# Row sums of transposed modulation weights on VectorE, and the gates' low halves moved from GpSimd to VectorE

## The chip, the cores and the metric

The kernel runs on one core of one Trainium2 chip. The metric is the device time of one execution in microseconds, the median of several runs. All input data are in HBM at the start, in the layouts that the host function `arrays` gives them; the host does no arithmetic.

## The reference, cut to what matters

Two diffusion blocks follow each other. Both scale, shift and gate their token streams by a modulation vector that is a product of a small activation with a wide matrix:

```python
silu_c = jax.nn.silu(c)
silu_cc = jax.nn.silu(c_ctx)[None]
for l in range(2):
    mod = silu_c @ w_ada[l] + b_ada[l]        # 1024 -> 6144, latent stream
    mod_c = silu_cc @ w_ada[l] + b_ada[l]     # the same for the context stream
    ...
    g = sigmoid(gate_cols)                    # 3 x 1024 columns of h @ w_in
    m = g[0]*(f_mix @ w_br_fourier) + g[1]*(o_g @ w_br_global) + g[2]*(o_w @ w_br_window)
    y = m @ w_out
    ...                                       # residual, then 16 experts
m_lat = jax.nn.silu(c_2) @ w_mod_2 + b_mod_2  # second block, 1024 -> 6144
```

In layer 1 the context stream needs only the first third of the modulation, and in the second block likewise, so for most of those two matrices only one of the two streams has to be modulated.

## The kernel before, in words

`build` runs `mixer(0)` (attention and branches of layer 0, both streams, 512 tokens), `moe(0)` (experts), `mixer(1)`, `moe(1)` and `block2`. A tile scheduler sets the order of the instructions on each engine when the kernel is built; the order in which the code issues them is the input to it.

Every weight matrix comes as blocks of 1 MB, [128, 2048] in fp32, into a ring of four raw buffers `w` (`raw`, line 176, and `wraw`, line 192). The loads stand in one queue, SyncE's, in the order in which the code asks for them, and a load starts only when the buffer four loads back has been read for the last time. Matrices that TensorE multiplies in two halves go through `halves` (line 180): ScalarE writes the high half `whi` (line 173), another engine the low half `wlo` as the difference (line 174). There are two buffer pairs for the halves, so a block is split while TensorE still works on the block before it. `mm3` (lines 163 to 165) then issues three matmuls per block of 128 rows.

Modulation comes in 36 chunks (m, c): matrix m (0 and 1 are the layers' `w_ada`, 2 is `w_mod_2`), columns 512c to 512c + 511. A chunk is two 1 MB loads. There are two ways to compute it:

- `mod_chunk` (line 263) on TensorE, for both streams.
- `mod_chunk_v` (line 285) on VectorE, for the latent stream alone. The weights lie with the input index on the partitions. Eight instructions on [128, 512] (one at line 298, seven at line 296) sum weight times activation into `modrow`, and four small matmuls against a column of ones (`one2`, issued through line 158) add over the partitions into a PSUM tile `sm`, of which there is a single one. Line 303 adds the bias.

`mixer(0)` gets a list `extra` of 32 chunks. Half of them run as fills between the steps of the two attentions, the other 16 in the strips of the branches: four strips jj, each with the gates (jj, 0..2), then a block of `wbr`, the branch products, and the merge on VectorE (lines 701 and 703). Four of the twelve gates, (0, 0), (0, 1), (0, 2) and (1, 0), are computed earlier, as fills in the attentions. Behind each gate's place some chunks are issued:

```python
load = [1 if x in early else 2 for x in order]
...
if (jj, i) not in early:
    gate(jj, i, nc.gpsimd if full else None)
n = 3 * jj + i
run_extra(round(len(extra) * load[n] / sum(load[n:])))
```

With `nc.gpsimd` the low halves of those eight gates are subtracted on GpSimd. Between the attentions and the strips stands `fourier` (line 542), a short chain of matmul, copy, matmul, copy. In front of the attentions stand five projections `proj` (line 397) of 256 columns each, from the blocks w_in 1024, 1280, 256, 512 and 768.

`bcast_cols` (line 317) spreads a column of 1024 values over all partitions as a row: eight matmuls against the identity (line 323) and two copies from PSUM (line 325).

Of the kernel before, what the change touches and what calls it, by code (L numbers as in the profile page):

```python
# [122 lines left out]
class Kernel:  # L123
# [89 lines left out]
    def setup(self):  # L213
        nc, tc, a = self.nc, self.tc, self.a
        st = self.st
        self.cp = st.enter_context(self.pool("consts"))
        self.pp = st.enter_context(self.pool("psum", space=PSUM))
        self.cw = {}
        nv = a["vecs"].shape[1]
        self.vec = self.cp.tile([128, nv], F32, name="vec")  # L220
        nc.sync.dma_start(self.vec, a["vecs"])
        self.ident = self.cp.tile([128, 128], F32, name="ident")
        nc.sync.dma_start(self.ident, a["ident"])
        self.ex = self.cp.tile([128, 1], F32, name="ex")
        nc.vector.memset(self.ex, -0.5)
        self.identb = self.cp.tile([128, 128], BF, name="identb")
        nc.vector.tensor_copy(self.identb, self.ident)
        self.ahead = {}
        self.one2 = self.cp.tile([128, 2], F32, name="one2")
        nc.vector.memset(self.one2, 1.0)  # L230
        self.modT = [self.cp.tile([128, 48, 2], F32, name=f"modT{i}") for i in range(3)]

        self.cst = []
        for i, nm in enumerate(("c", "c2")):
            c = self.V(nm).rearrange("p (s k) -> p s k", s=2)
            t = self.cp.tile([128, 2, KT], F32, name="silu")
            nc.scalar.activation(t, c, AF.Tanh, scale=0.5)
            nc.vector.scalar_tensor_tensor(t, t, 1.0, c, op0=OP.add, op1=OP.mult)
            s = self.cp.tile([128, KT, 32], F32, name=f"cst{i}")
            nc.vector.memset(s, 0.0)  # L240
            nc.vector.tensor_scalar(s[:, :, 0:2], t.rearrange("p s k -> p k s"), 0.5, None, op0=OP.mult)
            self.cst.append(s)
# [41 lines left out]

    def mod_chunk_v(self, m, c):

        nc = self.nc
        src = self.a["w_ada"][m] if m < 2 else self.a["w_mod_2"]
        st = self.cst[0 if m < 2 else 1]
        acc = self.mp.tile([128, 512], F32, name="modrow")  # L290
        for h in range(2):
            w = self.wraw(src[2 * c + h], 4, 512)
            for k in range(4):
                s = st[:, 4 * h + k, 0:1]
                if h or k:
                    nc.vector.scalar_tensor_tensor(acc, w[:, k], s, acc, op0=OP.mult, op1=OP.add)  # L296
                else:
                    nc.vector.tensor_scalar(acc, w[:, k], s, None, op0=OP.mult)
        pt = self.psum("sm", [128, 4, 2])
        for b in range(4):  # L300
            self.mm(pt[:, b], acc[:, b * 128:b * 128 + 128], self.one2, True, True)
        b = self.V("b_ada", m) if m < 2 else self.V("b_mod")
        nc.vector.tensor_tensor(self.modT[m][:, 4 * c:4 * c + 4], pt,
                                b[:, 4 * c:4 * c + 4].unsqueeze(2).to_broadcast([128, 4, 2]), op=OP.add)

    def mod_coef(self, m, i, gain, name, parts=1):
# [251 lines left out]
    def mixer(self, l, xsrc, extra):  # L558
# [9 lines left out]
        def run_extra(n):  # L568
            for _ in range(min(n, len(extra))):
                m, c = extra.pop(0)  # L570
                (self.mod_chunk_v if m and c >= 4 else self.mod_chunk)(m, c)

        gates = {}

        def gate(jj, i, eng=None):
            w = self.wsplit(a["w_in"][l, 6 + 4 * i + jj], eng)
            for j in range(2):
                ps = self.psum("pg")
                for k in range(KT):
                    self.mm3(ps[:, :N], [x[:, k, j * 128:j * 128 + 128] for x in w],  # L580
                             [h[:, k, :N] for h in self.hl], k == 0, k == KT - 1)
                g = gp.tile([128, N], F32, name="gate", bufs=8)
                nc.scalar.activation(g, ps[:, :N], AF.Tanh, scale=0.5)
                gates[jj, i, j] = g
# [1 line left out]

        early = [(0, 0), (0, 1), (0, 2), (1, 0)]
        fills = [lambda x=x: gate(*x) for x in early]
        at = len(extra) * 16 // 32
        for n in range(at):  # L590
            fills.insert(n * (len(fills) - n) // at + n, lambda: run_extra(1))
        rate = max(0, len(fills) - 2) / (6 * T)
# [33 lines left out]
        with self.pool(f"at{l}", side="right") as self.ap:  # L626
            self.consts(self.ap, _const_attn, "cattn")
            self.maskb = self.ap.tile([128, 256], BF, name="maskb")
            mask = self.ap.tile([128, 256], F32, name="mask", tag="rt2")
            nc.scalar.dma_start(mask, a["mask"])  # L630
            nc.vector.tensor_copy(self.maskb, mask)
            gq = self.ap.tile([128, 64], F32, name="gq")
            nc.gpsimd.dma_start(gq, a["q_norm_g"][l:l + 1].to_broadcast([128, 64]))
            gk = self.ap.tile([128, 64], F32, name="gk")
            nc.gpsimd.dma_start(gk, a["k_norm_g"][l:l + 1].to_broadcast([128, 64]))
            sink = self.ap.tile([128, 4], F32, name="sink")
            nc.gpsimd.dma_start(sink, a["sink"][l:l + 1].to_broadcast([128, 4]))
            z4 = self.ap.tile([128, T, 256], F32, name="z4")
            kvw = self.ap.tile([128, 4, 256], F32, name="kvw")
            heads = lambda x: x.rearrange("p t (h v d) -> p t h v d", v=2, d=64)  # L640
            qw = heads(z4)
            self.proj(l, 1024, lambda t: qw[:, t].rearrange("p h v d -> p v h d"), range(T))
            self.proj(l, 1280, lambda t: kvw[:, t], range(4))
            qv = z4.rearrange("p t (h d) -> p t h d", d=64)
            kv = kvw.rearrange("p t (h d) -> p t h d", d=64)
            for t in range(2):
                self.rope(qv[:, t], t)
                self.rope(kv[:, t, 0:2], t)
            qg = self.ap.tile([128, T, 512], F32, name="qg")
            qgh = heads(qg)  # L650
            kvg = self.ap.tile([128, 4, 256], F32, name="kvg")
            self.proj(l, 256, lambda t: qgh[:, t, :, 0], range(T))
            self.proj(l, 512, lambda t: qgh[:, t, :, 1], range(T))
            self.proj(l, 768, lambda t: kvg[:, t], range(4))
            self.attention(l, qw, kv, 2, T, lambda h, t: oT[:, 6 + h, t * 128:t * 128 + 128], fill, sink=sink)
            f = self.ap.tile([128, T, 256], F32, name="z4")
            self.proj(l, 0, lambda t: f[:, t], range(T))
            qv = qg.rearrange("p t (h d) -> p t h d", d=64)
            kv = kvg.rearrange("p t (h d) -> p t h d", d=64)
            for t in range(4):  # L660
                if t < T:
                    self.head_norm(qv[:, t], gq)
                self.head_norm(kv[:, t, 0:2], gk)
                if t < 2:
                    self.rope(qv[:, t], t)
                    self.rope(kv[:, t, 0:2], t)
            self.attention(l, qgh, kv, 4, T, lambda h, t: oT[:, 2 + h, t * 128:t * 128 + 128], fill)
            fill(len(fills))
            for s in range(S):
                self.fourier(f, s, lambda c: oT[:, c, s * 256:s * 256 + 256])  # L670
# [6 lines left out]
        with self.pool(f"br{l}", side="right") as bp:  # L677
# [1 line left out]
            for k in (6, 7, 2, 3, 4, 5, 0, 1):  # L679
                self.split(ol[0][:, k], ol[1][:, k], oT[:, k])  # L680
            order = [(jj, i) for jj in range(4) for i in range(3)]
            load = [1 if x in early else 2 for x in order]
            for jj in range(4):
                for i in range(3):
                    if (jj, i) not in early:
                        gate(jj, i, nc.gpsimd if full else None)
                    n = 3 * jj + i
                    run_extra(round(len(extra) * load[n] / sum(load[n:])))
                w = self.wsplit(a["wbr"][l, jj])
                for _ in range(EARLY[jj] if not full else 0):  # L690
                    self.load_expert(l, FIRST + len(self.pre))
# [1173 lines left out]
def _blocks(w, k, n):  # L1865


    *lead, r, c = w.shape
    m = len(lead)
    w = w.reshape(*lead, r // (128 * k), k, 128, c // n, n)  # L1870
    w = w.transpose(*range(m), m + 3, m, m + 2, m + 1, m + 4)
    return np.ascontiguousarray(w.reshape(*lead, -1, 128, k * n))
# [6 lines left out]

def _mod_blocks(w):  # L1880

    return np.concatenate([_blocks(w[:, :2048], KT, 256), _blocks(w[:, 2048:], 4, 512)])


def arrays(inp):
# [29 lines left out]
def build(tc, a, dbg=None):  # L1915
# [4 lines left out]
    k.wps, k.sps = [k.wp], [k.sp]  # L1920
    with k.pool("modp", bufs=2, side="right") as k.mp:
        k.mixer(0, [a["x"], a["ctx"]],
                     [(0, c) for c in range(4, 12)] + [(m, c) for r in (range(4), range(4, 12)) for m in (1, 2) for c in r])
    k.moe(0, 2, 2)
    k.dbg("xl0", k.X[0][:, 0])
    k.mixer(1, None, [])
# [23 lines left out]
```

## Time and profile before

| what | value |
|---|---|
| median of 3 runs | 2176.22 us (2176.04 to 2177.61) |
| the profiled execution | 2179.61 us, its span 2177.8 us |
| TensorE (PE) busy | 1911.4 us, 88% of the span, mean granted clock 0.92 |
| VectorE (DVE) busy | 986.0 us, 45% |
| ScalarE (ACT) busy | 546.9 us, 25% |
| GpSimd (POOL) busy | 115.5 us, 5% |
| DMA | 601.95 MB, mean 276 GB/s |
| costliest VectorE line of the chunks, L296 | 112 instructions, 105.4 us, mean 950 ns |

Busy shares are averages over the whole span. The layer-0 mixer takes the first quarter of it, and what a change there is worth has to be read from the windows, waits and timeline of that quarter. The granted clock is a share of full speed: 1.00 is 2.4 GHz, 0.50 is 1.2 GHz. PEld is the loading of weights into TensorE, which overlaps matmuls; PE's idle time in front of an instruction is given with what ended it.

### The profile page before, as it was taken

How to read it: one execution, taken by the hardware profiler on the slowest of the kernel's cores; microseconds unless marked ns; L12 is line 12 of the kernel's file. 1: busy time of each engine (PE TensorE's matmuls, PEld its weight loads, DVE VectorE, ACT ScalarE, POOL GpSimd, SP SyncE). 2: the span in 40 equal slices, each digit the busy share in tenths (PEclk: the TensorE clock that was granted, in tenths of full speed). 3: DMA queues.
4: the chain of work that ended last, by engine and by line, in shares of the span. 5: the costliest groups of instructions: out<-in, count | busy, mean ns of one | idle time of the engine just before them, and what ended most of it. 6: DMA issues, size and time to landing. Idle time of an engine off the chain costs nothing. (4 is left out here: it accounts for less than half of the span.)

```text
span 2177.8 us, 31443 instructions
## 1 busy us (share of the span) xinstructions
PE 1911.4 (88%) x13182; PEld 1288.5 (59%) x13182; DVE 986.0 (45%) x1907; ACT 546.9 (25%) x1076; POOL 115.5 (5%) x113
## 2 busy tenths in 40 slices
PE   5999999997999999787989977688876659998998
PEld 4967767886433343222968964354432228897997
DVE  3485688864222133123787642132221036855554
ACT  3144422231000110002344420131100014344342
POOL 0210013200000000000210000000000000100000
PEclk9999998998999989999999988888886778998999
DMA  8255766775799959999314669999899992313541
GB/s 331 76 217 212 271 232 251 283 298 203 296 421 420 410 223 420 420 421 385 135 59 155 239 232 418 419 391 421 338 416 420 417 393 98 117 59 121 187 177 59
DMA packets 85454, 601.95 MB, mean 276 GB/s; under 512 B 10048, under 2 KB 10848, under 8 KB 13376
## 3 DMA queue, kind: packets, MB, share of 16 engines
q1 hardware_dynamic: 82928, 594.15, 68.8%
q10 hardware_dynamic: 1840, 5.46, 0.7%
q8 instruction: 104, 1.70, 0.3%
q0 software_dynamic: 544, 0.32, 0.2%
q14 instruction: 38, 0.31, 0.0%
HBM read 598.84 MB, written 1.05 MB: 275 GB/s over the span
## 5 line engine op out<-in xcount | busy, mean ns | idle before, releaser
L158 PE MATMUL ps<-we 128*32 128x256 f32 (+2 forms) x2400 | 358.4, 528 | 88.1 <-DMA we<-w_up_e_dram 46.4
L158 PEld LDWEIGHTS ps<-we 128*32 128x32 f32 (+2 forms) x2400 | 124.5, 138 | 298.1 <-issue 118.2
L173 ACT CAST whi<-w 128x1024 fp32r<-128x1024 f32 x170 | 174.1, 1045 | 232.2 <-PE ps L164 110.0
L158 PE MATMUL ps<-we,gT 128*32 128x256 f32 (+1 forms) x1536 | 201.5, 494 | 30.7 <-DMA we<-w_down_e_dram 30.5
L174 DVE TENSOR_TENSOR wlo<-w,whi 128x1024 fp32r<-128x1024 f32 x154 | 185.8, 1220 | 84.7 <-ACT whi L173 84.1
L1022 DVE TENSOR_TENSOR we<-ps,we 32x512 f32<-32x512 f32 (+1 forms) x128 | 70.9, 554 | 209.4 <-PE ps L158 207.8
L158 PEld LDWEIGHTS ps<-we,gT 128*32 128x32 f32 (+1 forms) x1536 | 65.9, 126 | 140.5 <-issue 73.3
L163 PE MATMUL ps<-hhi,whi 128*128 128x512 f32 (+1 forms) x384 | 133.2, 347 | 0.1
L164 PE MATMUL ps<-hlo,whi 128*128 128x512 f32 (+1 forms) x384 | 132.5, 346 | 0.0
L165 PE MATMUL ps<-hhi,wlo 128*128 128x512 f32 (+1 forms) x384 | 131.6, 345 | 0.1
L296 DVE SCALAR_TENSOR_TENSOR modrow<-w,cst,modrow 128x512 f32<-128x512 f32 x112 | 105.4, 950 | 2.3
L158 PE MATMUL ps<-we,xg 128*32 128x256 f32 (+1 forms) x768 | 99.3, 484 | 5.3 <-DMA we<-w_gate_e_dram 3.6
L989 DVE TENSOR_TENSOR g<-tanh,ps 128x512 f32<-128x512 f32 (+1 forms) x32 | 17.7, 554 | 185.7 <-PE ps L158 185.6
L163 PE MATMUL ps<-hl,whi 128*128 128x256 f32 x352 | 100.6, 286 | 0.1
L165 PE MATMUL ps<-hl,wlo 128*128 128x256 f32 x352 | 99.9, 286 | 0.0
L164 PE MATMUL ps<-hl,whi 128*128 128x256 f32 x352 | 99.7, 285 | 0.0
L163 PE MATMUL ps<-whi,hhi 128*128 128x256 f32 x320 | 92.6, 291 | 2.5 <-DVE hhi L376 2.3
L986 ACT ACTIVATE tanh<-ps 128x512 f32<-128x512 f32 (+1 forms) x32 | 15.7, 490 | 312.0 <-PE ps L158 312.0
L164 PE MATMUL ps<-wlo,hhi 128*128 128x256 f32 x320 | 91.9, 289 | 0.9 <-DVE wlo L174 0.9
L987 DVE SCALAR_TENSOR_TENSOR tanh<-tanh,ps 128x512 f32<-128x512 f32 (+1 forms) x32 | 17.7, 554 | 165.3 <-ACT tanh L986 165.3
L165 PE MATMUL ps<-whi,hlo 128*128 128x256 f32 x320 | 91.2, 290 | 0.0
L210 POOL TENSOR_TENSOR rstd<-rstd,ex 128x2 f32<-128x2 f32 (+2 forms) x17 | 16.2, 954 | 1344.7 <-DVE rstd L342 1294.2
(423 smaller groups left out, 3557.9 us busy)
## 6 DMA issues: line engine op xcount, KB each, us to landing
we<-w_gate_e_dram SPq DMA_DIRECT2D x128, 1024.0 KB, 14.1
we<-w_up_e_dram SPq DMA_DIRECT2D x128, 1024.0 KB, 12.1
we<-w_down_e_dram SPq DMA_DIRECT2D x128, 1024.0 KB, 13.6
w<-w_in_dram SPq DMA_DIRECT2D x53, 1024.0 KB, 5.4
w<-w_ada_dram SPq DMA_DIRECT2D x48, 1024.0 KB, 5.5
w<-w_mod_dram SPq DMA_DIRECT2D x24, 1024.0 KB, 5.5
w<-w_out_dram SPq DMA_DIRECT2D x12, 1024.0 KB, 4.7
w<-w_gate_dram SPq DMA_DIRECT2D x11, 1024.0 KB, 4.7
```

Of the source, the lines that this page charges most:

```text
L158: self.nc.tensor.matmul(ps, l, r, start=first, stop=last)
L163: mm(ps, l[0], r[0], start=first, stop=False)
L164: mm(ps, l[0], r[1], start=False, stop=False)
L165: mm(ps, l[1], r[0], start=False, stop=last)
L173: self.nc.scalar.copy(hi, x)
L174: (eng or self.nc.vector).tensor_tensor(lo, x, hi.bitcast(F32), op=OP.subtract)
L210: self.nc.gpsimd.tensor_tensor(out, x, self.ex[:x.shape[0], e:e + 1].to_broadcast(list(x.shape)), op=OP.pow)
L296: nc.vector.scalar_tensor_tensor(acc, w[:, k], s, acc, op0=OP.mult, op1=OP.add)
L986: nc.scalar.activation(t, pa[:, :W], AF.Tanh, scale=0.5)
L987: nc.vector.scalar_tensor_tensor(t, t, 1.0, pa[:, :W], op0=OP.add, op1=OP.mult)
L989: nc.vector.tensor_tensor(g, t, pu[:, :W], op=OP.mult)
L1022: nc.vector.tensor_tensor(op[e // 4 % 2][p:p + 32, s, j * W:j * W + W], ps[i, :W], gb[s][i, j * W:j * W + W], op=OP.mult)
```

## The change

`mod_chunk_v` gets its weights transposed: 128 output columns on the partitions and all 1024 inputs along the row. One instruction per 128 columns multiplies such a row with the activation, spread over the partitions as a row `crow`, and accumulates the sum along the row into one column of `modcol`. Four such instructions make a chunk, and no matmul or PSUM is needed. The product is written back over the weights. `silu_row` makes `crow` with `bcast_cols`: once in front of the projections (into a part of `oT` that is free then) and twice, for both activations, in front of the strips.

The list is cut to 27 chunks. Chunks (1, 4) to (1, 8) run in the projections, one behind each; 16 run in the attentions as before; the last 11 run in strips 2 to 4, none in strip 1. The gates' low halves are no longer given to GpSimd, so VectorE computes them.

```diff
     def mod_chunk_v(self, m, c):
...
-        st = self.cst[0 if m < 2 else 1]
-        acc = self.mp.tile([128, 512], F32, name="modrow")
+        row = self.crow[0 if m < 2 else 1]
+        acc = self.mp.tile([128, 4, 1], F32, name="modcol")
         for h in range(2):
-            w = self.wraw(src[2 * c + h], 4, 512)
-            for k in range(4):
-                s = st[:, 4 * h + k, 0:1]
-                if h or k:
-                    nc.vector.scalar_tensor_tensor(acc, w[:, k], s, acc, op0=OP.mult, op1=OP.add)
-                else:
-                    nc.vector.tensor_scalar(acc, w[:, k], s, None, op0=OP.mult)
-        pt = self.psum("sm", [128, 4, 2])
-        for b in range(4):
-            self.mm(pt[:, b], acc[:, b * 128:b * 128 + 128], self.one2, True, True)
+            w = self.wraw(src[2 * c + h], 2, D)
+            for k in range(2):
+                nc.vector.scalar_tensor_tensor(w[:, k], w[:, k], 1.0, row, op0=OP.mult, op1=OP.mult,
+                                               accum_out=acc[:, 2 * h + k])
...
-        def gate(jj, i, eng=None):
-            w = self.wsplit(a["w_in"][l, 6 + 4 * i + jj], eng)
+        def silu_row(i, out):
+
+            self.crow[i] = out
+            self.bcast_cols(out, self.cst[i][:, :, 0])
+
+        def gate(jj, i):
+            w = self.wsplit(a["w_in"][l, 6 + 4 * i + jj])
...
-        at = len(extra) * 16 // 32
+        at = 16 if full else 0
...
+            if full:
+                silu_row(0, oT[:, 0:2].rearrange("p k n -> p (k n)"))
+            rows = iter(range(4, 9) if full else [])
+
+            def row_chunk():
+                for c in itertools.islice(rows, 1):
+                    self.mod_chunk_v(1, c)
+
             self.proj(l, 1024, lambda t: qw[:, t].rearrange("p h v d -> p v h d"), range(T))
+            row_chunk()
             self.proj(l, 1280, lambda t: kvw[:, t], range(4))
+            row_chunk()
...
-            load = [1 if x in early else 2 for x in order]
+            load = [0 if x in early else 1 for x in order]
+            if full:
+                for i in range(2):
+                    silu_row(i, bp.tile([128, D], F32, name=f"crow{i}"))
...
                     if (jj, i) not in early:
-                        gate(jj, i, nc.gpsimd if full else None)
+                        gate(jj, i)
                     n = 3 * jj + i
-                    run_extra(round(len(extra) * load[n] / sum(load[n:])))
+                    run_extra(round(len(extra) * load[n] / max(1, sum(load[n:]))))
```

How this moves instructions shows at three places. The first is SyncE's queue of loads for the projections (w_in are the projections' blocks, w_ada modulation). Before:

```order
L195 DMA w<-w_ada_dram 128x2048 x4
L195 DMA w<-w_in_dram 128x2048
L195 DMA w<-w_ada_dram 128x2048 x2
L195 DMA w<-w_in_dram 128x2048 x4
L195 DMA w<-w_ada_dram 128x2048 x8
```

and with the change:

```order
L195 DMA w<-w_ada_dram 128x2048 x4
L195 DMA w<-w_in_dram 128x2048
L195 DMA w<-w_ada_dram 128x2048 x4
L195 DMA w<-w_in_dram 128x2048
L195 DMA w<-w_ada_dram 128x2048 x2
L195 DMA w<-w_in_dram 128x2048
L195 DMA w<-w_ada_dram 128x2048 x2
L195 DMA w<-w_in_dram 128x2048
L195 DMA w<-w_ada_dram 128x2048 x2
L195 DMA w<-w_in_dram 128x2048
L195 DMA w<-w_ada_dram 128x2048 x10
```

Two modulation loads now stand between any two of the projections' blocks, where the last four of those stood together.

The second is TensorE from the end of the attentions into the first strip (fy, z and cattn are the Fourier mix, ohi and whi the first branch products, hhi and whi a gate, one the sums of modrow, modT and cst the rows of `bcast_cols`). Before:

```order
L158 MATMUL ps<-fy,cattn 128x256 x2
L158 MATMUL ps<-cattn,z_1558 128x512 x2
L158 MATMUL ps<-one_69,modrow 128x2 x4
L323 MATMUL ps<-ident,modT_71 128x128 x2
L158 MATMUL ps<-one_69,modrow 128x2 x4
...
L158 MATMUL ps<-fy,cattn 128x256 x2
L158 MATMUL ps<-one_69,modrow 128x2 x4
L163 MATMUL ps<-ohi,whi 128x512 x2
L164 MATMUL ps<-olo,whi 128x512 x2
```

and with the change:

```order
L158 MATMUL ps<-fy,cattn 128x256 x2
L158 MATMUL ps<-cattn,z_1618 128x512 x2
L163 MATMUL ps<-hhi,whi 128x512
L164 MATMUL ps<-hlo,whi 128x512
L165 MATMUL ps<-hhi,wlo 128x512
L163 MATMUL ps<-hhi,whi 128x512
L158 MATMUL ps<-fy,cattn 128x256 x2
L158 MATMUL ps<-cattn,z_1618 128x512 x2
L164 MATMUL ps<-hlo,whi 128x512
L165 MATMUL ps<-hhi,wlo 128x512
L163 MATMUL ps<-hhi,whi 128x512
L164 MATMUL ps<-hlo,whi 128x512
```

The sums of modrow are gone, the rows of modT have moved behind the strips, rows of cst have come, and 22 matmuls of gate (1, 1) now stand among the Fourier mix and ahead of the first branch product.

The third is VectorE from the end of strip 1 into strip 2 (mt and mT are the merge of the branches). Before:

```order
L703 TENSOR_TENSOR mT<-mt 128x512
L296 SCALAR_TENSOR_TENSOR modrow<-w,cst_77,modrow 128x512
L298 TENSOR_SCALAR modrow<-w,cst_77 128x512
L296 SCALAR_TENSOR_TENSOR modrow<-w,cst_77,modrow 128x512 x11
L303 TENSOR_TENSOR modT_72<-ps,vec 128x8 x2
L313 SCALAR_TENSOR_TENSOR n_1_9348<-modT_72,vec 128x16
L298 TENSOR_SCALAR modrow<-w,cst_77 128x512
L296 SCALAR_TENSOR_TENSOR modrow<-w,cst_77,modrow 128x512 x7
L174 TENSOR_TENSOR wlo<-w,whi 128x1024 x2
```

and with the change:

```order
L718 TENSOR_TENSOR mT<-mt 128x512
L174 TENSOR_TENSOR wlo<-w,whi 128x1024
L294 SCALAR_TENSOR_TENSOR w,modcol<-w,crow_3002 128x1024 x4
L174 TENSOR_TENSOR wlo<-w,whi 128x1024
L297 TENSOR_TENSOR modT_70<-modcol,vec 128x8
L174 TENSOR_TENSOR wlo<-w,whi 128x1024
L307 SCALAR_TENSOR_TENSOR n_1_9240<-modT_70,vec 128x16
L294 SCALAR_TENSOR_TENSOR w,modcol<-w,crow_3002 128x1024 x3
L174 TENSOR_TENSOR wlo<-w,whi 128x1024
```

The gates' low halves now stand in this queue, each behind up to four of the new instructions, and the addition of the bias no longer reads PSUM. From the block `w_out` on, all engines have the instructions of before in the same order.

## Rows read from the trace of the kernel before

**Rows 1.** Windows by stage: busy (instructions) of PE, PEld, DVE, ACT, POOL; PEclk, DMA share, GB/s.
```profile
42.00:110.00 68.00, 62.65 (x515) 61.08 (x519) 33.03 (x64) 16.81 (x30) 12.08 (x18) 0.95 0.34 127
282.00:297.00 15.00, 12.60 (x65) 8.80 (x63) 10.97 (x20) 7.36 (x13) 0.00 (x0) 0.96 0.60 211
297.00:458.00 161.00, 154.43 (x680) 126.58 (x680) 134.95 (x172) 33.60 (x42) 43.83 (x17) 0.93 0.72 274
```

**Rows 2.** Groups by line and form on PE, strips (297 to 458 us); busy us, mean ns.
```profile
L158 PE MATMUL ps<-one,modrow 128*128 128x2 f32 x104 | 14.2, 258 | 4.4 <-DVE modT L303 4.4
```

**Rows 3.** The same view on DVE, strips.
```profile
L296 DVE SCALAR_TENSOR_TENSOR modrow<-w,cst,modrow 128x512 f32<-128x512 f32 x91 | 89.9, 997 | 1.9
...
L298 DVE TENSOR_SCALAR modrow<-w,cst 128x512 f32<-128x512 f32 x12 | 6.9, 572 | 0.3 <-DMA w<-w_mod_dram 0.3
...
L303 DVE TENSOR_TENSOR modT<-ps,vec 128x8 f32<-128x8 f32 x13 | 2.1, 163 | 13.1 <-PE ps L158 13.0
```

**Rows 4.** Timeline of PE at the end of a gate: start us, us, instruction.
```profile
344.40 0.39 PE L164 MATMUL ps<-hlo,whi 128*128 128x512 f32 x1
344.63 0.40 PE L165 MATMUL ps<-hhi,wlo 128*128 128x512 f32 x1
344.87 0.95 PE L158 MATMUL ps<-one,modrow 128*128 128x2 f32 x8
345.68 0.48 PE L163 MATMUL ps<-ohi,whi 128*128 128x512 f32 x1
```

**Rows 5.** Waits of PE in the strips: total us, times, longest us.
```profile
PE ps L158 <- DVE modT L303: 4.4, 2, 2.7
...
PE ps L164 <- DVE olo L174: 1.5, 1, 1.5
```

**Rows 6.** Timelines of DVE, POOL and PE around the longer of those waits.
```profile
324.77 5.51 DVE L296 SCALAR_TENSOR_TENSOR modrow<-w,cst,modrow 128x512 f32<-128x512 f32 x2
330.20 0.15 DVE L303 TENSOR_TENSOR modT<-ps,vec 128x8 f32<-128x8 f32 x1
...
324.27 5.46 POOL L174 TENSOR_TENSOR wlo<-w,whi 128x1024 fp32r<-128x1024 f32 x2 [18.51 <-ACT whi L173]
...
330.41 1.87 PE L158 MATMUL ps<-one,modrow 128*128 128x2 f32 x8 [2.74 <-DVE modT L303]
```

**Rows 7.** Windows around the stretches at half clock, columns as in the first group.
```profile
282.00:295.60 13.60, 12.58 (x64) 8.78 (x62) 9.57 (x18) 5.96 (x10) 0.00 (x0) 1.00 0.56 189
295.80:305.80 10.00, 7.28 (x16) 5.25 (x17) 9.96 (x11) 3.63 (x6) 6.40 (x2) 0.50 0.43 180
...
330.00:336.50 6.50, 6.09 (x18) 5.18 (x19) 4.33 (x10) 0.00 (x0) 0.00 (x0) 0.50 0.86 325
...
371.00:377.50 6.50, 6.50 (x19) 5.46 (x20) 4.79 (x7) 1.99 (x2) 1.38 (x1) 0.50 1.01 402
```

**Rows 8.** DVE prices: whole-kernel groups by form, and line 918 alone (min/median/max ns).
```profile
L174 DVE TENSOR_TENSOR wlo<-w,whi 128x1024 fp32r<-128x1024 f32 x154 | 185.8, 1220 | 84.7 <-ACT whi L173 84.1 <-PE ps L1689 0.2
...
L721 DVE SCALAR_TENSOR_TENSOR mlo<-mT,mhi 128x512 fp32r<-128x512 f32 x8 | 4.9, 684 | 0.0
...
L918 DVE SCALAR_TENSOR_TENSOR affj<-ps,we x12: 414/421/425, 771.6 to 1526.6; 128x256 f32<-128x256 f32 x12
L918 DVE DVE_READ_ACCUMULATOR affj<-ps,we x12: 80/82/84, 772.0 to 1527.0; 128x1 f32 x12
```

**Rows 9.** Timeline of PE at another call of bcast_cols, at full clock.
```profile
1323.44 2.05 PE L323 MATMUL ps<-ident,modT 128*128 128x128 f32 x16
1325.39 0.44 PE L169 MATMUL ps<-ident,g 128*128 128x128 f32 x2
```

**Rows 10.** Timeline of PE in front of the projections.
```profile
44.15 0.58 PE L163 MATMUL ps<-whi,hhi 128*128 128x256 f32 x1 [2.26 <-DVE hhi L376]
```

**Rows 11.** Waits of PE behind the strips, 458 to 531 us.
```profile
PE ps L163 <- ACT mhi L720: 2.4, 1, 2.4
```

**Rows 12.** Waits of SyncE's queue for expert loads (L785), 445 to 545 us.
```profile
SPq L785 <- DVE wlo L174: 40.6, 4, 15.0
```

More of the change, by code (lines that the diff above doesn't have):

```diff
@@ L228, in setup @@
         self.ahead = {}
-        self.one2 = self.cp.tile([128, 2], F32, name="one2")
-        nc.vector.memset(self.one2, 1.0)
+        self.crow = {}
         self.modT = [self.cp.tile([128, 48, 2], F32, name=f"modT{i}") for i in range(3)]
@@ L288, in mod_chunk_v @@
         src = self.a["w_ada"][m] if m < 2 else self.a["w_mod_2"]
-        st = self.cst[0 if m < 2 else 1]
-        acc = self.mp.tile([128, 512], F32, name="modrow")
+        row = self.crow[0 if m < 2 else 1]
+        acc = self.mp.tile([128, 4, 1], F32, name="modcol")
         for h in range(2):
-            w = self.wraw(src[2 * c + h], 4, 512)
-            for k in range(4):
-                s = st[:, 4 * h + k, 0:1]
-                if h or k:
-                    nc.vector.scalar_tensor_tensor(acc, w[:, k], s, acc, op0=OP.mult, op1=OP.add)
-                else:
-                    nc.vector.tensor_scalar(acc, w[:, k], s, None, op0=OP.mult)
-        pt = self.psum("sm", [128, 4, 2])
-        for b in range(4):
-            self.mm(pt[:, b], acc[:, b * 128:b * 128 + 128], self.one2, True, True)
+            w = self.wraw(src[2 * c + h], 2, D)
+            for k in range(2):
+                nc.vector.scalar_tensor_tensor(w[:, k], w[:, k], 1.0, row, op0=OP.mult, op1=OP.mult,
+                                               accum_out=acc[:, 2 * h + k])
         b = self.V("b_ada", m) if m < 2 else self.V("b_mod")
-        nc.vector.tensor_tensor(self.modT[m][:, 4 * c:4 * c + 4], pt,
+        nc.vector.tensor_tensor(self.modT[m][:, 4 * c:4 * c + 4], acc.to_broadcast([128, 4, 2]),
                                 b[:, 4 * c:4 * c + 4].unsqueeze(2).to_broadcast([128, 4, 2]), op=OP.add)
@@ L652, in mixer @@
             self.proj(l, 256, lambda t: qgh[:, t, :, 0], range(T))
+            row_chunk()
             self.proj(l, 512, lambda t: qgh[:, t, :, 1], range(T))
+            row_chunk()
             self.proj(l, 768, lambda t: kvg[:, t], range(4))
+            row_chunk()
             self.attention(l, qw, kv, 2, T, lambda h, t: oT[:, 6 + h, t * 128:t * 128 + 128], fill, sink=sink)
@@ L1880, in _mod_blocks @@
 def _mod_blocks(w):
-    return np.concatenate([_blocks(w[:, :2048], KT, 256), _blocks(w[:, 2048:], 4, 512)])
+    n = w.shape[1] // 256
+    t = w.T.reshape(n, 2, 128, D).transpose(0, 2, 1, 3).reshape(n, 128, 2 * D)
+    return np.concatenate([_blocks(w[:, :2048], KT, 256), t[8:]])
 def arrays(inp):
@@ L1922, in build @@
         k.mixer(0, [a["x"], a["ctx"]],
-                     [(0, c) for c in range(4, 12)] + [(m, c) for r in (range(4), range(4, 12)) for m in (1, 2) for c in r])
+                     [(0, c) for c in range(4, 12)] + [(m, c) for m in (1, 2) for c in range(4)]
+                     + [(1, c) for c in range(9, 12)] + [(2, c) for c in range(4, 12)])
     k.moe(0, 2, 2)
```

## The prediction

> **What bounds the kernel now.** I read the windows by stage first, then for the strips the groups by line, the waits and the timeline. In the strips (297 to 458 us) TensorE is busy for 154.4 of 161 us and VectorE for 134.9, while the DMA engines carry 274 GB/s [rows 1]. TensorE sets the end there. Its gate matmuls follow each other every 0.23 us [rows 4], and only three things break this pace. One is the sums of modrow, 104 short matmuls in 13 chunks [rows 2]; a chunk's eight keep the next real matmul away for 345.68 - 344.87 = 0.81 us [rows 4]. The second is waits, 4.4 us of them for line 303, the bias addition that frees the one PSUM tile `sm` [rows 5]. The third is the clock: three stretches run at a granted 0.50, which is 1.2 GHz [rows 7].
>
> How these hang together shows in the timelines [rows 6]. Two instructions of line 296 take 5.51 us beside a GpSimd subtraction of 5.46 us, though the mean of all 91 in the strips is only 997 ns [rows 3]. Line 303 stands behind them and starts at 330.20; TensorE, whose next sums need the PSUM tile, starts at 330.41 after 2.74 us of idleness, and the first window at 0.50 behind it is 330.0 to 336.5 [rows 7]. The second such stretch, 371.0 to 377.5, follows the other wait of the same kind (4.4 - 2.7 = 1.7 us).
>
> In the projections (42 to 110 us) TensorE is busy for 62.7 of 68 us, VectorE for only 33.0, DMA at 0.34 [rows 1]: there is room for VectorE work and loads.
>
> **The change part by part.** The sum is against the profiled execution, 2179.6 us, which is 3.4 us above the median of 2176.2; I subtract that at the end.
>
> *Sums of modrow removed.* 16 chunks at 0.81 us [rows 4] are 13.0 us of TensorE, 13 of the chunks in the strips and 3 in the Fourier stretch before. All of it stands on TensorE's path: **-13.0**. The price at full clock is the lower one, so the bound is on the safe side.
>
> *Waits for line 303 removed.* The new bias addition reads SBUF, nothing on TensorE waits for it, and GpSimd has no subtractions left: **-4.4** [rows 5].
>
> *The clock behind them.* Two windows of 6.5 us at half speed lose 3.25 us each: **-6.5** [rows 7]. If another wait took their place, one of the two could stay, so the bound is -3.2.
>
> *The start of the strips.* From 282.0 to 295.6 TensorE idles for 13.6 - 12.6 = 1.0 us and from 295.8 to 305.8 for 10.0 - 7.3 = 2.7 us [rows 7], the latter waiting for the halves of the branch inputs [rows 5]. The order of the change puts 22 gate matmuls there, 22 x 0.23 = 5.1 us of work, which covers 3.7 us of idleness: **-3.7**. The 10 us at 0.50 lose 5.0 us. What the engine did before the fall was Fourier matmuls with idleness and short sums between; now dense gate matmuls stand in it. I take half, **-2.5**. Bounds for the whole start: -2 (a part of the idleness covered, clock as before) and -8.7.
>
> *Rows of silu added.* A `bcast_cols` occupies TensorE for 1325.39 - 1323.44 = 1.95 us [rows 9], and there are three: 5.9 us. Half of the one before the projections, 1.0 us, falls into the 2.26 us that TensorE idles there [rows 10]. The call for modT that stood in the Fourier stretch moves behind the strips to where TensorE waits 2.4 us for ScalarE anyway [rows 11]: 1.95 less here and nothing there, or 1.95 more if that wait doesn't cover it. Net **+2.9**, bounds +1.6 and +4.9.
>
> *Chunks in the projections.* A new instruction has two fp32 inputs from SBUF, 1024 wide, and an accumulated sum. The nearest rows are the subtraction of line 174, 1220 ns for 1024 with both inputs in SBUF, and line 918, which accumulates over 256 at 421 ns, with one input in PSUM, and an accumulator read of 82 ns behind it [rows 8]. I take 1.30 us, so a chunk is 4 x 1.30 + 0.16 (bias, [rows 3]) = 5.4 us. Five chunks and two copies of 0.68 bring VectorE from 33.0 to 61.2 of 68 us: not the bound. Ten more loads of 1 MB are 10.5 MB on top of 127 GB/s x 68 us = 8.6 MB, 280 GB/s, which the strips sustain now [rows 1]. But the projections' blocks now queue behind two modulation loads each, and low halves behind four instructions, 5.2 us, where a projection lasts some 13 us (the 68 us hold five). I put **+1.0** for it, bounds 0 and +6.
>
> *Chunks and low halves in the strips.* VectorE without lines 296, 298 and 303 has 134.9 - 89.9 - 6.9 - 2.1 = 36.0 us [rows 1, 3]. To it come 16 subtractions of 1.22 us (19.5), 11 chunks of 5.4 us (59) and four copies (2.7): 117 us, against about 161 - 10.5 - 4.4 - 6.5 - 3 = 137 us that TensorE then needs. That is 85% of a shorter stage, as 84% of the longer one before, so it stays covered on average. It is tight in strip 3, which gets five chunks: 5 x 5.4 + four blocks at 2.44 + ten merges at 0.68 = 43.6 us, against 4 x 48 x 0.23 = 44 us of TensorE. What would be late is the low half of a gate behind the chunks; the gate waits, and its ScalarE tanh and the next loads behind it. I allow **+2.0**, bounds 0 and +6.
>
> Sum: -13.0 - 4.4 - 6.5 - 6.2 + 2.9 + 1.0 + 2.0 = -24.2, so 2155.4 for such an execution and **2152 us** for the median. With every term at its good bound -31 (2145), with every term at its bad bound -13.0 - 4.4 - 3.2 - 2 + 4.9 + 6 + 6 = -5.7 (2170).
>
> **Does the gain survive?** From `w_out` on the order is the same on all engines. The expert loads behind the strips wait in the queue mostly for VectorE to release buffers, 40.6 us of it [rows 12], so they start earlier when the mixer ends earlier.
>
> **The rivals.**
>
> *Half rate: slower.* An accumulating instruction with two fp32 streams from SBUF might run at half rate per element. No row of before has such an instruction. From 684 ns at 512 and 1220 at 1024 [rows 8] an element costs 1.05 ns and the start 148 ns; at half rate the instruction would be 0.148 + 2 x 1.072 + 0.08 = 2.37 us and a chunk 9.6 us. VectorE would then need 33.0 + 1.4 + 48 = 82.4 us in the projections (+14.4) and 36 + 19.5 + 106 + 2.7 = 164 us in the strips (+3): **2194 us**. It decides from about 1.65 us per instruction, where the projections' VectorE reaches 68 us. Against it: line 918 accumulates at 421 ns, and without accumulation its width would take 684 - 256 x 1.05 = 415; and line 721, with both sources in SBUF and no accumulation, has the full rate [rows 8]. For it: line 918 reads one input from PSUM, so it doesn't test the case. The Trainium skill, "Vector Engine (DVE) Microarchitecture Reference", section "Points that are easy to get wrong", says that an instruction of this kind with two non-bf16 sources in SBUF halves throughput, since no port is left for the accumulator; by that rule the time is the 2194 us of this rival, and no run here shows the case yet. Chance 0.08.
>
> *A new wait in place of the old: faster by less.* In strips 3 and 4 a low half comes late behind four of the new instructions, TensorE stalls for about 5.2 us once in each strip, and the clock falls for 6.5 us after each, 3.25 us lost: 2 x 8.5 = 17 us given back, less the 2 allowed above, so 2152 + 15 = **2167 us**. For it: 43.6 against 44 us in strip 3. Against it: a gate's block can be split while the gate before it is multiplied, a lead of 11 us. Chance 0.14.
>
> *The gain is lost later: no change.* If the expert stream were bound by DMA from a fixed start, the 24 us would turn into waits in the first expert stage, **2176 us**. Against it stands the wait of the loads for buffers [rows 12]. Chance 0.04.
>
> **How the numbers follow.** The forecast has 0.74. What a measurement of this kernel can tell from no change is about 0.2%, 4.4 us. Faster: forecast and new wait, 0.88; same 0.04; slower 0.08. The range of 8 in 10 goes from 2144, a little under the good bounds, to 2168, which takes in most of the new-wait rival; the other two rivals and a rest are left out.
>
> **What would show it right or wrong.** Right: the stretch from 282 us to the end of the strips, 176 us before, about 150 us; no matmuls with one, no GpSimd subtractions; no wait of TensorE for modT; no window at 0.50 between the first branch product and the end of strip 4; the new instruction at 1.2 to 1.3 us; projections at most 2 us longer. The forecast is wrong if the new instruction takes over 1.65 us, if TensorE waits for wlo in the projections or in strips 3 and 4, or if the first expert stage gets longer by what the mixer gained.

## The result, and the profile after

The change runs in **2146.92 us** (median of 4, 2143.44 to 2147.62), the kernel before beside it in 2176.91 us: ratio 0.985, 95% interval 0.983 to 0.987. The forecast was 2152 us with a range of 2144 to 2168. The profiled execution of the change took 2146.93 us, span 2145.2 us, against 2179.61 and 2177.8 us: 32.6 us of span, where the sum had 24.2.

Windows of the change, for the Fourier mix and for the strips (columns as in [rows 1]):

```profile
284.31:300.09 15.78, 15.78 (x68) 11.04 (x67) 5.33 (x12) 5.69 (x11) 0.00 (x0) 1.00 0.20 66
300.09:428.00 127.91, 127.91 (x563) 104.90 (x563) 105.15 (x169) 31.10 (x40) 1.68 (x3) 1.00 0.77 295
```

Against [rows 1] TensorE has no idle time left here, the granted clock is 1.00 throughout instead of 0.93 in the strips, VectorE is busy for 82% of the strips (84% before), and GpSimd's 43.8 us are down to 1.7. Timeline of PE, the two matmuls that bound the stretch I compare all runs by, the first of the Fourier mix and the first of `w_out`:

```profile
284.31 1.03 PE L158 MATMUL ps<-fy,cattn 128*128 128x256 f32 x4
...
430.55 0.39 PE L163 MATMUL ps<-whi,mhi 128*128 128x256 f32 x1 [0.59 <-ACT mhi L735]
```

The stretch lasts 146.2 us; in the kernel before it went from 281.25 to 460.38 us, 179.1. That is a gain of 32.9 us, all of the difference in span. Its waits of PE, 281 to 461 us, in the change (there are no others; total us, times, longest):

```profile
PE ps L165 <- DVE mlo L736: 1.1, 1, 1.1
PE ps L163 <- ACT mhi L735: 0.6, 1, 0.6
```

None is in the strips; the 2.4 us for mhi of [rows 11] are 0.6, since the rows of modT now fill that gap. The new instruction, all of the change's strips by its line (min/median/max ns), and the group of its partner, the low halves, in the strips:

```profile
L294 DVE SCALAR_TENSOR_TENSOR w<-w,crow x44: 1216/1220/1226, 304.6 to 404.2; 128x1024 f32<-128x1024 f32 x44
L294 DVE DVE_READ_ACCUMULATOR w<-w,crow x44: 81/83/85, 305.7 to 405.4; 128x1 f32 x44
...
L174 DVE TENSOR_TENSOR wlo<-w,whi 128x1024 fp32r<-128x1024 f32 x22 | 26.5, 1221 | 13.1 <-ACT whi L173 13.1
```

The row sum costs what a plain subtraction of that width costs [rows 8], plus the read of the accumulator.

### The profile page after: what moved, and what is told of

Read it like the earlier page. It is cut to its first block, busy times and chain, and to the rows that moved or that the text cites. A ratio compares the mean times of both kernels' runs of the same rounds, so it can differ in the third digit from the quotient of the medians.

```text
span 2145.2 us, 31259 instructions
## 1 busy us (share of the span) xinstructions
PE 1891.1 (88%) x13102; PEld 1266.5 (59%) x13102; DVE 969.2 (45%) x1928; ACT 546.9 (25%) x1076; POOL 75.4 (4%) x97
## 5 line engine op out<-in xcount | busy, mean ns | idle before, releaser
L174 DVE TENSOR_TENSOR wlo<-w,whi 128x1024 fp32r<-128x1024 f32 x170 | 205.3, 1220 | 94.3 <-ACT whi L173 93.8
L158 PEld LDWEIGHTS ps<-P,xr 128*128 128x128 f32 x384 | 52.4, 203 | 59.5 <-issue 27.4
L1012 ACT ACTIVATE gT<-ps 128x512 f32<-128x512 f32 (+1 forms) x32 | 15.7, 490 | 278.5 <-PE ps L169 278.5
## 6 DMA issues: line engine op xcount, KB each, us to landing
we<-w_gate_e_dram SPq DMA_DIRECT2D x128, 1024.0 KB, 14.4
we<-w_down_e_dram SPq DMA_DIRECT2D x128, 1024.0 KB, 14.4
```

The source lines that it names most:

```text
L158: self.nc.tensor.matmul(ps, l, r, start=first, stop=last)
L174: (eng or self.nc.vector).tensor_tensor(lo, x, hi.bitcast(F32), op=OP.subtract)
```

## The experiments

The profiles give two numbers for each run: the time with its ratio to the kernel before on the same chip, and the stretch from the first Fourier matmul to the first of `w_out` in the profiled execution. The stretch is the sharper one: for the change, profiled twice, it was 146.24 us both times. The other runs were profiled once each, so that their stretches have no spread of their own. What lies behind the stretch has the same code in every run, and in the profiled executions it still took from 1710.0 us (c1) to 1723.3 us (a3); this is why totals are the blunter measure.

| run | us | ratio (95%) | stretch, us | at 0.50 in it, us |
|---|---|---|---|---|
| kernel before | 2176.91 | 1 | 179.1 | 23.9 |
| a1: low halves on VectorE | 2168.75 | 0.996 (0.994 to 0.997) | 168.4 | 10.2 |
| a2: no sums | 2163.75 | 0.993 (0.991 to 0.996) | 166.3 | 13.7 |
| a3: both | 2155.86 | 0.989 (0.986 to 0.992) | 153.7 | 6.8 |
| a4: both, and none in strip 1 | 2149.52 | 0.986 (0.983 to 0.989) | 152.4 | 3.4 |
| a5: none in strip 1, alone | 2183.96 | 1.002 (1.000 to 1.004) | 182.0 | 20.5 |
| the change | 2146.92 | 0.985 (0.983 to 0.987) | 146.2 | 0 |
| b1: low halves on GpSimd | 2160.29 | 0.992 (0.989 to 0.995) | 156.5 | 3.4 |
| b2: row sums twice | 2200.42 | 1.010 (1.007 to 1.013) | 179.0 | 23.9 |
| b3: chunks in strip 1 too | 2165.87 | 0.994 (0.991 to 0.996) | 165.2 | 13.7 |
| b4: none in projections | 2161.20 | 0.992 (0.989 to 0.995) | 161.3 | 6.8 |
| b5: short matmuls put back | 2162.17 | 0.993 (0.991 to 0.995) | 156.1 | 0 |
| c1: rows by DMA | 2145.52 | 0.984 (0.981 to 0.986) | 143.8 | 0 |
| the change again, beside c1 | 2144.54 | 0.983 (0.981 to 0.986) | 146.2 | 0 |

**GpSimd or the sums.** The first three runs start from the kernel before. Run a1:

```diff
-                        gate(jj, i, nc.gpsimd if full else None)
+                        gate(jj, i)
```

> The kernel before, with the gates' low halves on VectorE instead of GpSimd, and nothing else. Theory S (the sums on TensorE are the main cost, GpSimd matters only through the two waits behind it): the waits for the bias addition (4.4 us) and the two windows at half clock behind them (6.5 us) go, the sums stay: about 2166 us, ratio 0.995, no instruction of the chunk's accumulation over 0.8 us. Theory G (GpSimd beside VectorE is the main cost): more than half of the 30 us comes from here, 2160 us or less. Theory N (the waits move elsewhere, since VectorE gets 16 subtractions more): 2174 us or more.

The time and the stretch (10.7 us shorter) are those of theory S: 4.4 us of waits and two windows at half clock. The accumulating line by itself, in the kernel before and then in a1:

```profile
L296 DVE SCALAR_TENSOR_TENSOR modrow<-w,cst,modrow x112: 737/752/2966, 269.1 to 442.3; 128x512 f32<-128x512 f32 x112
```

```profile
L296 DVE SCALAR_TENSOR_TENSOR modrow<-w,cst,modrow x112: 741/751/753, 268.3 to 428.8; 128x512 f32<-128x512 f32 x112
```

Run a2 takes out the matmuls instead:

```diff
-        pt = self.psum("sm", [128, 4, 2])
-        for b in range(4):
-            self.mm(pt[:, b], acc[:, b * 128:b * 128 + 128], self.one2, True, True)
+        pt = acc[:, 0:8].rearrange("p (b r) -> p b r", r=2)
```

> The kernel before without the matmuls against the column of ones: the bias addition reads the first eight columns of modrow, so the sum over the partitions of 16 chunks is left out. Low halves stay on GpSimd. Theory S: the sums (13.0 us), the waits for the PSUM tile (4.4 us) and the clock behind them (6.5 us) go: about 2153 us, although instructions of 2 to 3 us beside GpSimd are still there. Theory G: the slowed instructions hold up something else in the strips, only the 13 us go: 2163 us or more.

Theory S missed by 11 us; theory G had 2163 us or more. The waits of PE in a2, and the timelines of DVE, POOL and PE around the longest:

```profile
PE ps L163 <- DVE mt L699: 7.8, 6, 3.1
...
336.91 4.34 DVE L296 SCALAR_TENSOR_TENSOR modrow<-w,cst,modrow 128x512 f32<-128x512 f32 x3
341.17 0.68 DVE L699 SCALAR_TENSOR_TENSOR mt<-gate,ps 128x512 f32<-128x512 f32 x1
...
334.18 4.95 POOL L174 TENSOR_TENSOR wlo<-w,whi 128x1024 fp32r<-128x1024 f32 x2 [14.28 <-ACT whi L173]
...
341.90 0.50 PE L163 MATMUL ps<-ohi,whi 128*128 128x512 f32 x1 [3.10 <-DVE mt L699]
```

With the PSUM tile `sm` gone, TensorE now waits for the merge, which frees the branch products' PSUM and stands behind the slowed instructions. The wait had not been removed, only its place had changed. Run a3 has both edits.

> Both edits on the kernel before: no sums over partitions (left out) and the gates' low halves on VectorE. Theory S: no more than 3 us below the run without sums alone, so 2150 to 2154 us; what then is missing to the change (2147 us) is the start of the strips, where the chunks of strip 1 stand. Theory G: at least 6 us below the run without sums alone.

The stretch is 25.5 us shorter, and a1 and a2 give 10.7 + 12.8 = 23.5: the two halves of the change add up, which is theory G and not S. The same from the other end, in run b1, which puts the low halves back on GpSimd in the change:

```diff
-        def gate(jj, i):
-            w = self.wsplit(a["w_in"][l, 6 + 4 * i + jj])
+        def gate(jj, i, eng=None):
+            w = self.wsplit(a["w_in"][l, 6 + 4 * i + jj], eng)
...
-                        gate(jj, i)
+                        gate(jj, i, nc.gpsimd if full else None)
```

> The change with the gates' low halves back on GpSimd. The run of the kernel before without sums had a new wait in place of the old, 7.8 us of TensorE for the merge. Theory W (GpSimd beside VectorE costs wherever TensorE needs VectorE next): TensorE waits for the merge or for low halves, 5 to 10 us, with one or two windows at half clock: 2154 to 2160 us. Rival S (row sums feed nothing that TensorE waits for, so slowed instructions are free): no such wait, 2145 to 2149 us.

Theory W holds: the stretch is 10.3 us longer. Waits of PE in it (all of them in the strips), and the timelines of DVE, POOL and PE at the longest:

```profile
PE ps L163 <- DVE mt L716: 7.9, 3, 4.0
...
374.77 3.47 DVE L294 SCALAR_TENSOR_TENSOR w<-w,crow 128x1024 f32<-128x1024 f32 x1
...
378.17 3.38 DVE L294 SCALAR_TENSOR_TENSOR w<-w,crow 128x1024 f32<-128x1024 f32 x1
...
382.62 0.68 DVE L716 SCALAR_TENSOR_TENSOR mt<-gate,ps 128x512 f32<-128x512 f32 x1
...
374.75 2.40 POOL L174 TENSOR_TENSOR wlo<-w,whi 128x1024 fp32r<-128x1024 f32 x1 [16.01 <-ACT whi L173]
...
377.11 3.35 POOL L174 TENSOR_TENSOR wlo<-w,whi 128x1024 fp32r<-128x1024 f32 x1
...
383.35 0.80 PE L163 MATMUL ps<-ohi,whi 128*128 128x512 f32 x1 [3.97 <-DVE mt L716]
```

Two row sums of 1.22 us become 3.47 and 3.38 beside two GpSimd subtractions of 2.40 and 3.35 us, and the merge behind them is late. Their ends come in turn: GpSimd at 377.15, VectorE at 378.24, GpSimd at 380.46, VectorE at 381.55 us. Each row sum ends 1.09 us behind a subtraction, so most of its work is done only after it. The Trainium skill, "SBUF — State Buffer", section "SBUF: two separate sides", has VectorE and GpSimd take a shared port pair in turn, whole instructions at a time, and this trace agrees. Run b5 prices the short matmuls in the change:

```diff
+        pt = self.psum("sm", [128, 4, 2])
+        for b in range(4):
+            self.mm(pt[:, b], self.ident, acc[:, 3].to_broadcast([128, 2]), True, True)
```

> The change, with four short matmuls of 128x2 put back behind every row-sum chunk (they read the chunk's last column, and nothing reads what they write). Theory S: 16 x 0.81 = 13 us on TensorE, 2160 us, TensorE's clock in strips 2 to 4 as in the change. Rival C (the short matmuls are what lets the clock fall): 2160 us and at least one stretch at 0.50 of 3.3 us cost more in the strips, 2163 to 2167 us. Rival F (they fit into gaps): under 2152 us.

The stretch grows by 9.8 us for its 11 chunks, 0.89 us each (0.81 in [rows 4]; a chunk's four matmuls are eight instructions in the trace), with no new wait and no half clock in it. The short matmuls cost their own time and do not bring the clock down; rival C falls.

**The rate of the row sum.** Run b2:

```diff
-            for k in range(2):
+            for k in (0, 0, 1, 1):
```

> The change with every row-sum instruction issued twice, 2.6 us in place of 1.3, which is about what half rate would have been; the first of the pair overwrites the weights, so the sums of the chunks are not what they should be. VectorE would need 65 + 26 = 91 us in projections of 78, and 105 + 57 = 162 us in strips of 128. Theory: VectorE becomes the bound in both, +14 and +34 us, 2190 to 2200 us, so slower than before, and the point of decision of the half-rate rival was right. Rival: only the projections or only the strips give, 2160 to 2182 us.

The upper end of the expectation was right: about what half rate would have cost, 54 us above the change, and slower than before. The wait of TensorE in the strips is then for low halves:

```profile
PE ps L165 <- DVE wlo L174: 17.4, 3, 7.8
PE ps L163 <- ACT whi L173: 4.5, 4, 2.4
```

**Where the chunks stand.** Run b3 gives strip 1 its chunks back:

```diff
-            load = [0 if x in early else 1 for x in order]
+            load = [1 if x in early else 2 for x in order]
```

> The change with the last 11 chunks spread as before, strip 1 included. Gate (1, 1) then no longer stands among the Fourier mix. Theory P (the start of the strips is worth 8 us because gate (1, 1) fills it): TensorE waits for ohi, olo and fy again, 4 to 5 us, and a window of 6.8 to 10 us at half clock is back at the first branch product: 2153 to 2156 us. Rival: VectorE's load is more even and nothing is lost, 2145 to 2149 us.

Theory P has the sign and under half of the size: the stretch is 19.0 us longer. Waits of PE, 280 to 440 us:

```profile
PE ps L317 <- DVE crow L319: 4.8, 2, 3.6
PE ps L163 <- ACT whi L173: 3.4, 1, 3.4
PE ps L165 <- DVE wlo L174: 1.7, 1, 1.7
PE ps L158 <- ACT fy L546: 0.7, 1, 0.7
```

These are 10.6 us, the 13.7 us at 0.50 lose 6.8, and the rows of modT (1.95 us) stand in the middle of the stretch again, where in the change they fill the gap in front of `w_out`: 19.4. What I had not expected is the first row: the matmuls of `crow` wait for its copy, which stands behind `olo` on VectorE. Run b4 takes the chunks out of the projections:

```diff
-            rows = iter(range(4, 9) if full else [])
+            rows = iter([])
...
-                     + [(1, c) for c in range(9, 12)] + [(2, c) for c in range(4, 12)])
+                     + [(1, c) for c in range(4, 12)] + [(2, c) for c in range(4, 12)])
```

> The change with no chunk in the projections and all 16 in strips 2 to 4. VectorE in the strips then needs 105 + 27 = 132 us against 128 of TensorE. Theory V: VectorE is the bound there, TensorE waits for the merge or for low halves: the projections give back 2 to 4 us, the strips lose 6 to 12, 2150 to 2157 us. Rival: VectorE has enough slack ahead of strip 2 and the projections' price was paid for nothing, 2142 to 2146 us.

Theory V has the sign, and the loss is larger than I had it: the stretch is 15.1 us longer. Its window of the strips, the waits of PE there, and the timelines of PE, ACT and SyncE at one of them:

```profile
298.44:441.60 143.16, 135.33 (x579) 108.22 (x578) 128.43 (x214) 31.27 (x40) 1.68 (x3) 0.98 0.85 325
...
PE ps L163 <- ACT whi L173: 6.5, 4, 1.6
...
380.70 0.50 PE L163 MATMUL ps<-ohi,whi 128*128 128x512 f32 x1 [1.62 <-ACT whi L173]
...
379.11 0.60 ACT L582 ACTIVATE gate<-ps 128x512 f32<-128x512 f32 x1 [4.39 <-PE ps L165]
379.61 3.88 ACT L173 CAST whi<-w 128x1024 fp32r<-128x1024 f32 x4
...
370.60 0.33 SPq L195 DMA_DIRECT2D w<-wbr_dram  x1
```

The block of `wbr` for the same strip in the change:

```profile
372.90 0.40 PE L163 MATMUL ps<-ohi,whi 128*128 128x512 f32 x1
...
363.48 2.00 ACT L173 CAST whi<-w 128x1024 fp32r<-128x1024 f32 x2 [0.66 <-DMA w<-wbr_dram]
...
356.88 0.33 SPq L195 DMA_DIRECT2D w<-wbr_dram  x1
```

VectorE is 90% busy, but the longest waits are for a high half, which is ScalarE's. In the change this block's load is issued 16 us ahead of its product and its cast runs 9 us ahead. In b4 the load is issued 10 us ahead; it has landed by 377.0 us, since such loads took at most 6.4 us, but the cast stands behind the tanh of the last gate, and that waits for TensorE. All four waits for whi in the strips have this pattern. They come of the later load and of the cast's place in ScalarE's queue, which is fixed when the kernel is built; no run separates the two. A load starts only when the block four loads back has been read, and in b4 more of those blocks are read by row sums. SyncE's waits for these in the strips, in b4 and then in the change:

```profile
SPq L195 <- DVE w L294: 89.4, 27, 23.1
```

```profile
SPq L195 <- DVE w L294: 64.8, 18, 23.1
```

In all b4 has 7.8 us of idleness in the strips, 3.4 of clock and the rows of modT again; some 2 us stay unassigned. Runs a4 and a5 put the new spread into a3 and into the kernel before:

```diff
-            load = [1 if x in early else 2 for x in order]
+            load = [0 if x in early else 1 for x in order]
```

> The kernel before without sums over partitions (left out) and with the low halves on VectorE, as in the run of both edits, and now with no chunk in strip 1, so that gate (1, 1) stands among the Fourier mix. Theory P: the start of the strips is filled, 4.7 us of waits and a window of 6.8 us at half clock go, about 8 us less than the run of both edits: 2146 to 2149 us. Rival V: 13 chunks in three strips hold up the blocks' loads as 16 did in the change without chunks in the projections: the 8 us are given back, 2153 to 2160 us.

> The kernel before with the new spread of the chunks alone, none in strip 1; sums and low halves on GpSimd as before. Theory P: the start is worth 8 us by itself, 2168 to 2170 us. Rival V: the chunks are denser in strips 2 to 4, where GpSimd slows them, and TensorE waits longer for the bias addition there: 2174 us or more.

By its median a4 comes to theory P, but a3's runs spread from 2147 to 2159 us, and the stretch is only 1.3 us shorter than a3's; the other difference between the two profiled executions lies behind `w_out`, 1714.0 us against 1723.3, and is none of the edit's. The start is filled as expected, and TensorE waits in the strips instead, 3.4 us for whi and 2.1 for wlo, with 3.4 us at 0.50: the loss is rival V's, though it is not shown that the loads cause it. In a5 it is plain, the waits of PE in the strips being

```profile
PE ps L158 <- DVE modrow L296: 7.4, 3, 3.4
PE ps L158 <- DVE modT L303: 4.2, 2, 2.3
```

so the spread alone is worth nothing or less. With the 13 chunks that the trace of a4 has in the strips TensorE waits even without GpSimd's work; with the change's 11, of another instruction, it does not.

**A version to beat both.** Run c1 on the change, with `crows` a new input that holds the two rows:

```diff
-            self.bcast_cols(out, self.cst[i][:, :, 0])
+            nc.gpsimd.dma_start(out, a["crows"][i:i + 1].to_broadcast([128, D]))
+            nc.scalar.activation(tmp, out, AF.Tanh, scale=0.5)
+            nc.vector.scalar_tensor_tensor(out, tmp, 1.0, out, op0=OP.add, op1=OP.mult)
```

> A version meant to beat both: the rows of the activation come by a DMA that spreads one row over the partitions, with tanh on ScalarE and one VectorE instruction, so that the 24 matmuls and six copies of the three rows go. Theory: TensorE has 3 x 1.95 = 5.9 us less on its path, of which 1.0 us is given back where it idles before the projections: 2142 us, 5 us below the change. Rival: the new ScalarE and VectorE work of 1 to 1.3 us per row stands ahead of work that TensorE needs at the start of the kernel and of the strips: no difference within 2 us.

> The change once more, as the yardstick for the run beside it: 2143 to 2149 us. Where the stretches at half clock fall in the first 300 us differed between runs of identical code, worth up to 4 us.

The two medians are 1 us apart within ranges of 3 and 6 us: no difference. The stretch did lose 2.4 us, but the start was later: the first projection matmul comes at 36.66 us instead of 34.52. The wait of PE in front of it, 0 to 36 us, in c1 and then in the change beside it:

```profile
PE ps L272 <- DMA w<-w_ada_dram: 10.0, 2, 9.7
```

```profile
PE ps L272 <- DMA w<-w_ada_dram: 7.8, 2, 7.2
```

In the other profile of the change the two numbers are 35.63 and 8.2 us, and without this DMA no run has the matmul later than 35.98 us, so that 0.7 to 2.1 us of the delay may come from the half a megabyte of the first row, moved at the very start. That it does is not shown; asking for the row later was not tried.

## Why the prediction was right, and where its sizes were off

*Sums of modrow, -13.0.* Right: 0.89 us a chunk when put back (b5), and with the low halves already on VectorE their removal shortens the stretch by 14.7 us, 1.7 of it clock (a1 to a3). The 12.8 us of a2 are not their price: they also hold a new wait and 10.2 us less at half clock.

*Waits for line 303, -4.4, and the clock behind them, -6.5.* The sum of 10.9 is what a1 gains, 10.7. The step that failed here is the reason I put first, that the bias addition "reads SBUF, nothing on TensorE waits for it". This removes the wait by name only: in a2 and b1, where nothing on TensorE waits for a chunk, the merge is late by 7.8 and 7.9 us in its place. What removed the wait is the second half of that sentence, that GpSimd has no subtractions left.

*Start of the strips, -3.7 and -2.5.* Under-sized. The windows of the stretch before:

```profile
281.25:297.00 15.75, 13.35 (x69) 9.48 (x67) 11.38 (x22) 7.36 (x13) 0.00 (x0) 0.96 0.62 221
297.00:457.83 160.83, 154.27 (x680) 126.58 (x680) 134.78 (x172) 33.43 (x42) 43.83 (x17) 0.93 0.72 273
```

TensorE idles for 15.75 - 13.35 up to 297 us and 160.83 - 154.27 after it, 9.0 us in all, of which 4.4 + 3.7 were in the sum; all of it went. So did all three windows at 0.50, 10.2 + 6.8 + 6.8 us, which lost half of it, 11.9; I had 9.0, taking half for the first. The sum's own 13.0 with these gives 33.9; less the net 1.3 us that rows cost in the stretch (below) it is 32.6 against 32.9 measured. But b3, a4 and a5 show that the new spread brings this only together with the five chunks in the projections and the quiet GpSimd.

*Strips, +2.0.* Nothing was given back: no wait for wlo or anything else. The estimate of VectorE's share, 85%, came out at 82%. In a4 (13 chunks, 124.7 of 134.2 us, 93%) and b4 (90%) VectorE is busier and TensorE waits, though less for the low halves that I feared (2.1 and 1.0 us) than for high halves (3.4 and 6.5).

*Projections +1.0 and rows of silu +2.9.* From the first projection matmul to the first score matmul a2, a3 and a4 take 71.86 us, b1 and b3 (with the change's code up to there) 73.42, all without half clock: +1.6 for the five chunks and the first row. From there to the Fourier mix, again without half clock, 171.75 us before and 172.36 in b1: +0.6, for half of the second row stands there. The other half and the third row stand in the stretch, 24 matmul instructions, 2.9 us by [rows 9], with two more for modT, 0.2, while the wait for mhi got 1.8 us shorter: +1.3. Together 3.5 where I had 3.9. The price of the chunks in the projections bought what b4 lost, 15.1 us.

*What the sum did not have.* In the stage of `w_out` TensorE ran at 0.50 for 10.2 us before and for 3.4 after; its windows before and in the change:

```profile
460.38:525.73 65.35, 63.94 (x481) 59.89 (x482) 27.09 (x42) 17.18 (x46) 0.00 (x0) 0.92 0.43 163
```

```profile
430.55:493.83 63.28, 61.89 (x481) 58.03 (x482) 27.12 (x42) 17.18 (x46) 0.00 (x0) 0.97 0.43 163
```

The 2.1 us are not an effect of the change that I can show; they are less than what runs of the same code differ by from there on (1710.0 to 1723.3 us).

*Does the gain survive.* It does: from the first matmul of `w_out` to the end 2177.8 - 460.38 = 1717.4 us before and 2145.2 - 430.55 = 1714.7 after.

*The rivals.* Half rate fell with the 1220 ns. The Trainium skill, "Vector Engine (DVE) Microarchitecture Reference", section "Points that are easy to get wrong", would have had the instruction at half throughput with two such sources; the trace says otherwise, and the measurement decides. Its price was near in total, b2 gives 2200 us where the rival had 2194, but by luck in its parts: against the kernel before, b2 takes 22.0 us longer from the first projection matmul to the Fourier mix and 0.2 less in the stretch, where the rival had 14.4 and 3. The new wait in strips 3 and 4 did not come; waits of 5.5 to 7.9 us with the clock behind them do come, for the merge or for halves, as soon as GpSimd (b1) or more chunks (a4, b4) are added.

## What to carry to other kernels

When a wait goes because its waiter is removed, look for what else stands behind the slow instruction on the same engine; the stall goes only when the instruction is fast again. Work moved to an engine with slack is worth what its place in the engines' queues and in the load ring allows: five chunks in the projections, with a row, cost 1.6 us there and saved 15 in the strips, while the new spread without that relief was worth nothing. And compare runs by a stretch between two named instructions where the total is noisier than the effect.

## What the runs showed of the hardware

- A multiply of two fp32 SBUF operands with an accumulated sum runs at the rate of the plain subtraction: 1220 ns for 1024 elements, and 83 ns for the read of the accumulator.
- Behind a wait of TensorE the clock fell (b1: idle for 3.97 us up to 383.35, granted 0.50 from there for 3.4 us); a scatter of 88 short matmul instructions in 11 chunks without waits did not bring it down (b5).
- Where the half clock falls in the first 300 us is not fixed by the code. The change in its first profile had two stretches of 3.4 us, at 36.8 and 111.9 us, and came to the Fourier mix at 284.31 us; in its second it had 10.2 us at 14.7 and 6.8 us at 106.8, and came there at 282.80. b1, with the same code up to there, had only the one at 14.7 us, where TensorE is busy for 4.3 of 11 us, and came there at 280.52.
